# Encoder block on one core: operands of the first up-projection round split and ordered anew, down-projection loads chained

## The chip, the cores and the metric

The kernel runs on 1 core of one Trainium2 chip. The metric is the device time in microseconds (us) of one launch. The engines are named as in the profile: PE (TensorE, matmuls), PEld (its weight loads), DVE (VectorE), ACT (ScalarE), POOL (GpSimd) and SP (SyncE, which issues DMAs here).

## What is computed

One encoder block over 1024 tokens of width 1024: a token mixer (convolution group and attention group), a cross-attention into 256 memory tokens, and a gated MLP. The change lies in the last step of the cross-attention, in the gated MLP and in nothing ahead of them. Cut to that:

```python
# D_MODEL = 1024, SEQ = 1024, D_FF = 2816
y = memory_cross_attention(h, mem_n, w_mem_q, w_mem_kv, w_mem_o)
x = x + rmsnorm(y, norm_mem_post)
h = rmsnorm(x, norm_ffn_pre)
u = jnp.einsum("bsd,df->bsf", h, w_up)          # 1024 -> 2 * 2816
u = dwconv_centred(u, ffn_dw, ffn_dw_b)          # width 3 over tokens
gate, val = u[..., :D_FF], u[..., D_FF:]
y = jnp.einsum("bsf,fd->bsd", gelu(gate) * val, w_down)
x = x + rmsnorm(y, norm_ffn_post)
```

All is float32.

## The kernel before

**Products.** A float32 operand is split into a high half (a cast to the fp32r type, on ACT) and a low half (the operand less its high half, a subtraction on DVE or POOL). A product of two operands is three matmuls for each slice of 128 rows: high by high, high by low, low by high (`gemm3`, lines 98, 99 and 101). A `product` of the up projection is four slices, so 12 matmuls of 128x512.

**Cross-attention's last step.** A loop over eight tiles of 128 tokens, `t` = 0 to 7. `cross_gemm(t)` multiplies (the matmuls `y<-Uw,P`), `cross_norm(t)` makes two RMS norms: a square with a running sum on ACT (L621, then L725), a scale and a power on POOL (`rsqrt`, L86 and L87), a scale on DVE (L623, then L727) and, between the two norms, the residual's addition on DVE (L624). `cross_operands(t)` turns the result on PE (`pTs`) and stores it in tiles `r_b` for the up projection.

**Up projection.** It is done with seven products instead of eight (Strassen and Winograd), in 22 rounds `fi`. The weights of a round are loaded as `wg` and `wv`, sums of them (`s`, L813 to L816, on POOL) and their halves (`a`, L780 on ACT, L781 on POOL or DVE) are the operands on the left. The operands on the right are made once from the tokens: b11, b21 (tiles 0 to 3 of `t`), b22, t1, t2, t3, t4 (tiles 4 to 7), each with halves `h` and `l`. In `cross_operands(t)` for `t` = 4 to 7 each piece of 128 tokens is subtracted (L713) and split (L709, L710) on its own. t3 and t4 lie in the buffers of the raw b12 and b21. A round is `up_first` (products with b11 and b21), `up_operands` (the halves) and `up_finish` (t1, t2, b22, t3, t4, the convolution, the gate and the store of the result to `act_d`, L869). The products' sums are added on DVE (L805, L842); there are four PSUM buffers of that kind, and the next product waits until the addition has read its buffer. While round `fi` is finished, `down_sums` (L773, four subtractions of 128x256 each round, on DVE) makes sums of the down projection's weights.

**Down projection.** Seven products m1, m2, m6, m7, m5, m4, m3 over 11 slices `i`; each slice takes 12 matmuls `yd` (L91 to L93) with one operand tile `op`: the left part is cast from `acts` (the stored gate results, loaded at L903 and L906 to L908), the right part from `st`, which one DMA brings for two slices (L924). The buffer of `st` is taken in turn from the pool `raw` (3 buffers) and the pool `tmp` (4 buffers, shared with the sums `s` and the gate results `o`).

**What sets the order.** A scheduler orders the instructions of every engine from its own estimate of when each could run. `tc.issue_after(x)` ties the instructions inside it behind `x`; `tc.high_priority()` lets them go ahead.

Of the kernel before, what the change touches and what calls it, by code (L numbers as in the profile page):

```python
# [34 lines left out]
def encoder_block(ctx: ExitStack, tc: tile.TileContext, x, xT, mem, w_a, w_q, w_kv, w_mkv, w_mqT,  # L35
# [668 lines left out]

    def b_split(name, ts_):
# [3 lines left out]
        nc.scalar.copy(out=hi[:, :, ts_], in_=src[:, :, ts_])  # L709
        nc.vector.tensor_tensor(out=lo[:, :, ts_], in0=src[:, :, ts_], in1=f(hi[:, :, ts_]), op=ALU.subtract)  # L710
# [18 lines left out]

    def cross_operands(t, j):  # L730
        h, tt = t // 4, t % 4
# [47 lines left out]
    def a_split(dst, src, eng):  # L779
# [27 lines left out]

    def up_operands(fi):

        rg, u, q = firsts.pop(fi)  # L810
        rv = load_raw(w_up[fi, 1], "wv")
        s12, s34 = tmp("s12"), tmp("s34")
        nc.gpsimd.tensor_tensor(out=s12[:, H0], in0=rv[:, H0], in1=rv[:, H1], op=ALU.add)  # L813
        nc.gpsimd.tensor_tensor(out=s12[:, H1], in0=s12[:, H0], in1=rg[:, H0], op=ALU.subtract)
        nc.gpsimd.tensor_tensor(out=s34[:, H0], in0=rg[:, H0], in1=rv[:, H0], op=ALU.subtract)
        nc.gpsimd.tensor_tensor(out=s34[:, H1], in0=rg[:, H1], in1=s12[:, H1], op=ALU.subtract)  # L816
        a2, a3 = W([2, 2, 512], "a2"), W([2, 2, 512], "a3")
        a_split(a2[:, 0], s12[:, H1], nc.vector)
        a_split(a2[:, 1], s12[:, H0], nc.vector)
        a_split(a3[:, 0], s34[:, H1], nc.vector)  # L820
        lo = a_split(a3[:, 1], s34[:, H0], nc.vector)
# [50 lines left out]
    for t in range(8):
        if t == 6:
            for fi in range(UP_PRE):
                rgs[fi] = load_raw(w_up[fi, 0], "wg")
# [4 lines left out]
        cross_operands(t, j)  # L880
    for fi in range(NF + 1):
        if fi < NF:
# [3 lines left out]
            lo = up_operands(fi)  # L886
            down_load(fi)
        if fi:
            up_finish(fi - 1)
        else:  # L890
            down_sums(0, lo)
# [25 lines left out]
    def right(name, i):  # L917

        if i % 2 == 0:
# [199 lines left out]
```

## Time and profile of the kernel before

| | us |
|---|---|
| median of 3 runs | 1430.79 |
| lowest, highest | 1429.89, 1430.89 |
| the profiled execution: its time | 1431.57 |
| its span | 1429.8 |
| PE busy | 1376.8 (96% of the span) |
| DVE busy | 1099.9 (77%) |
| ACT busy | 699.5 (49%) |
| POOL busy | 527.1 (37%) |
| mean granted clock of PE, as a share | 0.988 |

The span is the profiled execution's stretch between the first and the last instruction; what lies around it is 1431.57 - 1429.8 = 1.77 us. In the views below a row of the timeline names a start, a duration, the engine, the line, the operation and the tiles (out<-in); in brackets stands how long the engine had been idle before, and whose work ended that. Rows of the same kind that follow each other are merged (x4). Matmuls overlap: one lasts longer than the distance to the next start.

### The profile page before, as it was taken

What the parts mean: (1) busy time and instruction counts of PE and PEld (TensorE: products, weight loads), DVE (VectorE), ACT (ScalarE), POOL (GpSimd) and SP (SyncE); (2) the same over time, 40 slices, a digit from 0 to 9 for tenths busy, and PEclk for the clock granted to TensorE, in tenths of its full rate; (3) what the DMA queues carried; (4) which work ended last, traced back from release to release, by engine and by line L of the source; (5) the groups of instructions that cost most, each with busy time, mean ns of one, the idle gap of its engine ahead of it and who ended that gap; (6) DMA issues with size and microseconds to landing.
All of it is one profiled execution on the core that took longest, in us unless ns stands there. A gap on an engine that the chain in (4) does not pass through costs nothing.

```text
span 1429.8 us, 18873 instructions
## 1 busy us (share of the span) xinstructions
PE 1376.8 (96%) x7042; PEld 1164.9 (81%) x7042; DVE 1099.9 (77%) x1443; ACT 699.5 (49%) x1190; POOL 527.1 (37%) x505
## 2 busy tenths in 40 slices
PE   9999999889999999999997999999999997999997
PEld 7889987679898888888885788888888886888885
DVE  6699899799999433435449989898898998696576
ACT  7426653678888444334335444444434444354452
POOL 5538877801011433102126455555555540000002
PEclk9999999999999999999998999999999998999998
DMA  7417760000000433203222443334444449523326
GB/s 239 138 50 230 244 224 14 21 1 1 30 1 1 148 104 133 74 32 116 88 89 88 162 147 133 121 130 147 133 147 147 148 148 331 212 82 96 103 89 213
DMA packets 77228, 170.08 MB, mean 119 GB/s; under 512 B 10065, under 2 KB 32849, under 8 KB 77137
## 3 DMA queue, kind: packets, MB, share of 16 engines
q1 hardware_dynamic: 77136, 168.88, 35.5%
q8 instruction: 55, 0.90, 0.2%
q14 instruction: 37, 0.30, 0.1%
HBM read 124.82 MB, written 44.04 MB: 118 GB/s over the span
## 4 chain that ended last, share of the span: by engine, by line
PE 69%; DVE 4%; DMA 2%; ACT 1%; issue 1%; POOL 1%; SPq 0%; POOLq 0%; DVEq 0%; ACTq 0%
PE p L101 9%; PE p L99 9%; PE p L98 9%; PE yd L91 5%; PE yd L92 5%; PE yd L93 5%; PE y L99 4%; PE y L101 4%; PE y L98 4%; PE pPT L82 3%; PE sc L101 2%; PE sc L98 2%; PE sc L99 2%; PE sp L536 2%; PE po L567 2%; PE sp L537 2%
## 5 line engine op out<-in xcount | busy, mean ns | idle before, releaser
L305 DVE SCALAR_TENSOR_TENSOR cacc<-conv,col,cacc 128x1009 f32<-128x1009 f32 (+14 forms) x120 | 145.8, 1275 | 4.8 <-ACT cacc L253 4.5
L86 POOL TENSOR_SCALAR rt<-ss 128x1 f32<-128x1 f32 (+1 forms) x43 | 14.9, 346 | 364.9 <-DVE ss L935 238.8
L92 PE MATMUL yd<-op 128*128 128x512 f32 x308 | 120.8, 393 | 0.0
L93 PE MATMUL yd<-op 128*128 128x512 f32 x308 | 120.6, 392 | 0.0
L91 PE MATMUL yd<-op 128*128 128x512 f32 x308 | 101.1, 393 | 9.1 <-ACT op L945 9.1
L945 ACT CAST op<-acts 128x512 fp32r<-128x512 f32 x77 | 47.8, 623 | 109.9 <-PE yd L93 99.5
L781 POOL TENSOR_TENSOR a<-wg,a 128x512 fp32r<-128x512 f32 x44 | 68.4, 1576 | 62.3 <-ACT a L780 62.3
L935 DVE TENSOR_TENSOR op<-acts,op 128x512 fp32r<-128x512 f32 x77 | 52.8, 688 | 46.7 <-ACT op L945 46.6
L781 DVE TENSOR_TENSOR a<-s,a 128x512 fp32r<-128x512 f32 x88 | 87.8, 1037 | 0.0
L831 ACT ACTIVATE c<-u,col 128x1024 f32<-128x1024 f32 x44 | 53.2, 1209 | 66.5 <-DVE u L842 66.5
L557 DVE TENSOR_TENSOR PL<-pPT,PH 128x512 fp32r<-128x512 f32 x128 | 83.1, 680 | 2.3 <-ACT PH L556 1.3
L539 DVE TENSOR_REDUCE nm<-sp 128x1 f32<-128x1024 f32 x64 | 78.0, 1218 | 7.4 <-PE sp L537 6.9
L780 ACT CAST a<-s 128x512 fp32r<-128x512 f32 x88 | 50.2, 619 | 64.8 <-DVE o L868 50.0
L842 DVE TENSOR_TENSOR u<-p,u 128x512 f32<-128x512 f32 x110 | 75.1, 683 | 7.2 <-PE p L101 6.2
L542 ACT ACTIVATE P<-sp,nm 128x1024 f32<-128x1024 f32 x64 | 72.1, 1126 | 15.4 <-PE pPT L82 6.5
L832 DVE SCALAR_TENSOR_TENSOR c<-u,col,c 128x1023 f32<-128x1023 f32 x44 | 56.5, 1285 | 28.8 <-ACT c L831 28.8
L556 ACT CAST PH<-pPT 128x512 fp32r<-128x512 f32 x128 | 69.4, 594 | 14.1 <-PE pPT L82 13.6
L91 PEld LDWEIGHTS yd<-op 128*128 128x128 f32 x308 | 58.5, 190 | 21.6 <-ACT op L945 9.5
L781 POOL TENSOR_TENSOR a<-wv,a 128x512 fp32r<-128x512 f32 x22 | 33.4, 1517 | 114.0 <-ACT a L780 112.9
L92 PEld LDWEIGHTS yd<-op 128*128 128x128 f32 x308 | 58.4, 190 | 12.7 <-DVE op L935 0.4
L82 PE MATMUL pPT<-ident,P 128*128 128x128 f32 x512 | 67.9, 273 | 0.7 <-DVE PL L557 0.7
L93 PEld LDWEIGHTS yd<-op 128*128 128x128 f32 x308 | 58.4, 190 | 12.2
(343 smaller groups left out, 4378.8 us busy)
## 6 DMA issues: line engine op xcount, KB each, us to landing
wg<-in_w_up_dram SPq DMA_DIRECT2D x22, 512.0 KB, 4.6
wv<-in_w_up_dram SPq DMA_DIRECT2D x22, 512.0 KB, 4.4
wd<-in_w_down_dram SPq DMA_DIRECT2D x22, 512.0 KB, 5.5
T_d<-wd SPq DMA_DIRECT2D x22, 512.0 KB, 3.2
act_d<-o SPq DMA_DIRECT2D x22, 512.0 KB, 3.1
acts<-act_d SPq DMA_DIRECT2D x44, 256.0 KB, 6.4
st<-T_d SPq DMA_DIRECT2D x20, 512.0 KB, 3.7
wmkv_r<-in_w_mkv_dram SPq DMA_DIRECT2D x16, 512.0 KB, 4.2
```

The source lines that it names most:

```text
L82: nc.tensor.transpose(out=out_, in_=in_, identity=ident)
L91: nc.tensor.matmul(out=ps, lhsT=sh, rhs=mh, start=first, stop=False)
L92: nc.tensor.matmul(out=ps, lhsT=sh, rhs=ml, start=False, stop=False)
L93: nc.tensor.matmul(out=ps, lhsT=sl, rhs=mh, start=False, stop=last)
L98: nc.tensor.matmul(out=p, lhsT=sh, rhs=mh, start=first, stop=False)
L99: nc.tensor.matmul(out=p, lhsT=sh, rhs=ml, start=False, stop=False)
L101: ins = nc.tensor.matmul(out=p, lhsT=sl, rhs=mh, start=False, stop=last)
L305: nc.vector.scalar_tensor_tensor(out=acc[:, t0:t1_], in0=a[:, t0 + o:t1_ + o], scalar=cc(C_DW + c * 31 + j), in1=acc[:, t0:t1_], op0=ALU.m ...
L539: nc.vector.reduce_max(out=nm, in_=sp, axis=AX.X, negate=True)
L557: nc.vector.tensor_tensor(out=PL[dst], in0=p3, in1=f(PH[dst]), op=ALU.subtract)
L781: return eng.tensor_tensor(out=dst[:, 1, :], in0=src, in1=f(dst[:, 0, :]), op=ALU.subtract)
L842: return nc.vector.tensor_tensor(out=dst, in0=other if swap else ps, in1=ps if swap else other, op=op)
```

## The change

**Right operands.** t3 and t4 are no longer split for each token tile. After the loop each is cast and subtracted once, on 128x2048, tied behind the last split of the others (t2's for the last tile). From `t` = 6 on the third subtraction (t3) goes to DVE instead of POOL.

**Left operands of the first rounds.** Round 0's weights are loaded at `t` = 3 and its sums made on POOL there. Round 1's go into a buffer `gv`. `up_weights`, `up_sums` and `up_seconds` are functions of their own; the low halves of rounds 0 and 1 on POOL are tied behind the last power of a norm, the `a2` halves behind the norm's square and scale. `cross_norm(7)` is made at high priority after round 0's `up_first`. Round 1's sums go to DVE, behind round 0's seventh product; `down_sums` of rounds 0 and 1 go behind round 0's gate.

**Down projection.** The loads of `st` are chained, each tied behind the load before it in the program. The first three take `raw` buffers, and from the fourth on odd ones take `raw` and even ones `tmp`.

```diff
+        last_pow[0] = nc.gpsimd.tensor_tensor(out=out_, in0=t, in1=mhalf[:, :n], op=ALU.pow)
...
     def cross_operands(t, j):
+        third = nc.gpsimd if t < 6 else nc.vector
...
-            b_sub("t3", "b22", "b12", ts_, nc.gpsimd)
+            b_sub("t3", "b22", "b12", ts_, third)
             b_sub("t2", "b22", "t1", ts_, nc.vector)
             b_split("t2", ts_)
-            b_split("t3", ts_)
             b_sub("t4", "t2", "b21", ts_, nc.vector)
-            b_split("t4", ts_)
...
+    def up_weights(fi, hi_at=None, lo_at=None):
         rg = rgs.pop(fi) if fi in rgs else load_raw(w_up[fi, 0], "wg")
         a1 = W([2, 2, 512], "a1")
-        a_split(a1[:, 0], rg[:, H0], nc.gpsimd)
-        a_split(a1[:, 1], rg[:, H1], nc.gpsimd)
+        a_split(a1[:, 0], rg[:, H0], nc.gpsimd, hi_at, lo_at)
+        a_split(a1[:, 1], rg[:, H1], nc.gpsimd, hi_at, lo_at)
+        weights[fi] = rg, a1
...
-        if fi + 1 < NF:
+        if 0 < fi < NF - 1:
             down_sums(fi + 1, seventh)
+        if fi == 0:
+            up_weights(2, last_hi[0])
+            with tc.issue_after(seventh.ins):
+                up_sums(1, firsts[1][0], nc.vector)
+                up_operands(1)
...
     UP_PRE = 2
+    PRE_T = 3
     for t in range(8):
-        if t == 6:
-            for fi in range(UP_PRE):
-                rgs[fi] = load_raw(w_up[fi, 0], "wg")
-        j = cross_norm(t, *cross_gemm(t))
-        if t == 7:
-            for fi in range(UP_PRE):
-                up_first(fi)
+        if t == PRE_T:
+            rgs[0], rvs[0] = load_raw(w_up[0, 0], "wg"), load_raw(w_up[0, 1], "wv")
+        y, xr = cross_gemm(t)
+        if t < 7:
+            j = cross_norm(t, y, xr)
+            if t == PRE_T:
+                up_sums(0, rgs[0])
+        else:
+            gv = wp.tile([128, 2, 1024], F32, tag="w", name="gv")
+            rgs[1], rvs[1] = gv[:, 0], gv[:, 1]
+            for i in range(2):
+                last_load[0] = nc.sync.dma_start(out=gv[:, i], in_=w_up[1, i])
+            up_weights(0, lo_at=last_pow[0])
+            up_first(0)
+            with tc.high_priority():
+                j = cross_norm(t, y, xr)
+            up_weights(1, lo_at=last_pow[0])
+            up_seconds(0, last_sq[0], last_h[0])
+            up_first(1)
         cross_operands(t, j)
...
-            lo = up_operands(fi)
+            if fi != 1:
+                up_operands(fi)
+            if fi == 0:
+                hi, lo = last_hi[0], last_lo[0]
+                with tc.issue_after(hi.ins), tc.issue_after(lo.ins):
+                    for n in ("t3", "t4"):
+                        b_split(n, slice(0, 512))
...
+        if fi == 1:
+            for n in range(2):
+                down_sums(n, gated)
...
-            st = (tmp if nst[0] % 2 == 0 else raw)("st").rearrange("p (i n) -> p i n", i=2)
-            ld = nc.sync.dma_start(out=st[:, :n, :], in_=src[i:i + n, :, b, :].rearrange("i p n -> p i n"))
-            pair[0] = st
+            st = (raw if nst[0] % 2 or nst[0] == 2 else tmp)("st").rearrange("p (i n) -> p i n", i=2)
+            with tc.issue_after(last_load[0].ins):
+                ld = nc.sync.dma_start(out=st[:, :n, :], in_=src[i:i + n, :, b, :].rearrange("i p n -> p i n"))
+            pair[0], last_load[0] = st, ld
```

The three places where the order of instructions moves, as the two programs issue them. (The numbers in tile names differ between the programs; `r_b_7058` before and `r_b_7068` after are t3's buffer, `r_b_6641` is t4's, `r_b_7059` and `r_b_7069` are t2's.)

DVE, end of the first round's operands, before (`a_7461`, `a_7462` are halves for round 0, `a_7487`, `a_7488` for round 1):

```order
L713 TENSOR_TENSOR r_b_7059<-r_b_7059,r_b_6640 128x4x128
L710 TENSOR_TENSOR t3l<-r_b_7058,t3h 128x4x128 x4
L713 TENSOR_TENSOR r_b_6641<-r_b_7059,r_b_6641 128x4x128
L781 TENSOR_TENSOR a_7462<-s_7456,a_7462 128x512
L710 TENSOR_TENSOR t2l<-r_b_7059,t2h 128x4x128
L710 TENSOR_TENSOR t4l<-r_b_6641,t4h 128x4x128 x4
L781 TENSOR_TENSOR a_7487<-s_7481,a_7487 128x512 x2
L781 TENSOR_TENSOR a_7488<-s_7482,a_7488 128x512 x2
L842 TENSOR_TENSOR u<-p_7500,u 128x512
```

The same place after (`a_7447` holds halves for round 0, `s_7529` and `s_7530` are round 1's sums):

```order
L714 TENSOR_TENSOR t1l<-r_b_6640,t1h 128x4x128
L717 TENSOR_TENSOR r_b_7069<-r_b_7069,r_b_6640 128x4x128
L820 TENSOR_TENSOR u<-p_7398,u 128x512
L717 TENSOR_TENSOR r_b_6641<-r_b_7069,r_b_6641 128x4x128
L714 TENSOR_TENSOR t2l<-r_b_7069,t2h 128x4x128
L790 TENSOR_TENSOR a_7447<-s_6978,a_7447 128x512 x2
L714 TENSOR_TENSOR t3l<-r_b_7068,t3h 128x2048
L873 TENSOR_TENSOR u<-p_7465,u 128x512
L714 TENSOR_TENSOR t4l<-r_b_6641,t4h 128x2048
L873 TENSOR_TENSOR u<-p_7466,u 128x512
```

The four pieces of t3l stood ahead of t2l and of the rest; now t2l and round 0's halves come first, t3l and t4l are one instruction each, and round 1's sums and halves stand behind them.

POOL, last token tile and first round, before:

```order
L713 TENSOR_TENSOR r_b_7058<-r_b_7059,r_b_7058 128x4x128
L781 TENSOR_TENSOR a_7393<-wg,a_7393 128x512 x2
L86 TENSOR_SCALAR rt_7355<-ss 128x1
L87 TENSOR_TENSOR rs<-rt_7355,mhalf 128x1
L813 TENSOR_TENSOR s_7455<-wv 128x512
L815 TENSOR_TENSOR s_7456<-wg,wv 128x512
L814 TENSOR_TENSOR s_7455<-s_7455,wg 128x512
L713 TENSOR_TENSOR r_b_7058<-r_b_7059,r_b_7058 128x4x128
L816 TENSOR_TENSOR s_7456<-wg,s_7455 128x512
```

and after (`a_7334` is round 0's, `a_7386` round 1's left operand for b11 and b21):

```order
L790 TENSOR_TENSOR a_7334<-wg,a_7334 128x512 x2
L88 TENSOR_SCALAR rt_7372<-ss 128x1
L89 TENSOR_TENSOR rs<-rt_7372,mhalf 128x1
L88 TENSOR_SCALAR rt_7382<-ss 128x1
L89 TENSOR_TENSOR rs<-rt_7382,mhalf 128x1
L790 TENSOR_TENSOR a_7386<-gv,a_7386 128x512 x2
L790 TENSOR_TENSOR a_7452<-wv,a_7452 128x512
L790 TENSOR_TENSOR a_7452<-gv,a_7452 128x512
L790 TENSOR_TENSOR a_7524<-wg,a_7524 128x512 x2
```

Round 1's low halves (before `a_7393`, ahead of the last norm's second power) now stand behind both powers of the last norm; the eight sums of rounds 0 and 1 that stood here are gone from it.

SP, last rounds of the up projection, before (`st_10612`, issued 29 rows earlier, is m1's first load; `st_10648` its second, `st_10726` its fourth, `st_10845` m2's first):

```order
L924 DMA st_10845<-in_w_down_dram 128x2x512
L906 DMA acts_10598<-act_d_6642 128x512
L869 DMA act_d_6642<-o_10494 128x1024
L910 DMA gF_10604<-in_rows_dram 128x1024
L907 DMA acts_10598<-act_d_6642 128x512
L908 DMA acts_10598<-act_d_6642 128x512
L907 DMA acts_10600<-act_d_6642 128x512
L907 DMA acts_10602<-act_d_6642 128x512
L906 DMA acts_10600<-act_d_6642 128x512
L908 DMA acts_10600<-act_d_6642 128x512
L924 DMA st_10648<-in_w_down_dram 128x2x512
L924 DMA st_10726<-in_w_down_dram 128x2x512
```

and after (`st_10635` is m1's second load, `st_10671` its third):

```order
L982 DMA st_10599<-in_w_down_dram 128x2x512
L960 DMA acts_10569<-act_d_6642 128x512
L780 DMA T_d_6643<-wd_6644 512x1x256
L960 DMA acts_10571<-act_d_6642 128x512
L960 DMA acts_10573<-act_d_6642 128x512
L960 DMA acts_10575<-act_d_6642 128x512
L905 DMA act_d_6642<-o_10336 128x1024
L982 DMA st_10635<-in_w_down_dram 128x2x512
L982 DMA st_10671<-in_w_down_dram 128x2x512
```

m1's second load stood behind its third, its fifth and m2's first, and behind the next to last store to `act_d`; now it follows its first with six rows between and stands ahead of the last two stores. ACT, at the end of m1 after (`op_10843`, `op_10863`, `op_10885` are m2's first three operands, `u_10593` m1's result; before, three whole operands of m2 stood ahead of these copies):

```order
L1003 CAST op_10843<-acts_10569 128x512
L1003 CAST op_10805<-st_10797 128x512
L1003 CAST op_10863<-acts_10571 128x512
L1003 CAST op_10885<-acts_10573 128x512
L1070 COPY u_10593<-yd_10595 128x512
L1070 COPY u_10593<-yd_10596 128x512
L1070 COPY u_10593<-yd_10597 128x512
L1070 COPY u_10593<-yd_10598 128x512
L1003 CAST op_10905<-acts_10575 128x512
L1003 CAST op_10843<-st_10832 128x512
L1003 CAST op_10863<-st_10832 128x512
```

The casts from `st` for m2's first operands stand behind the four copies of m1's result.

## Rows read from the trace of the kernel before

**Rows 1.** Page, part 1: busy time, share of the span, instructions of each engine.

```profile
PE 1376.8 (96%) x7042; PEld 1164.9 (81%) x7042; DVE 1099.9 (77%) x1443; ACT 699.5 (49%) x1190; POOL 527.1 (37%) x505
```

**Rows 2.** Waits of PE from 740 to 842 us: whom for, total, times, longest.

```profile
PE p L99 <- DVE t3l L710: 3.8, 1, 3.8
PE pTs L82 <- DVE h L727: 3.4, 2, 2.3
PE p L98 <- ACT t1h L709: 3.1, 1, 3.1
PE p L99 <- DVE t1l L710: 1.9, 1, 1.9
```

**Rows 3.** Windows: from:to, us, busy of PE, PEld, DVE, ACT, POOL; PEclk, DMA share, GB/s.

```profile
756.01:841.00 84.99, 71.74 (x295) 56.72 (x294) 79.30 (x89) 40.01 (x64) 51.81 (x37) 0.90 0.37 124
1197.40:1419.00 221.60, 212.50 (x926) 175.03 (x924) 158.03 (x258) 98.19 (x183) 10.40 (x13) 0.98 0.44 150
```

**Rows 4.** Timeline of PE, first round of the up projection.

```profile
757.45 1.06 PE L82 MATMUL pTs<-ident,h 128*128 128x128 f32 x8 [1.06 <-DVE h L727]
758.27 0.48 PE L98 MATMUL p<-b11h,a 128*128 128x512 f32 x1
...
763.84 0.39 PE L98 MATMUL p<-b11h,a 128*128 128x512 f32 x1
...
789.00 0.80 PE L99 MATMUL p<-t3l,a 128*128 128x512 f32 x1 [3.82 <-DVE t3l L710]
...
793.86 0.63 PE L101 MATMUL p<-b22h,a 128*128 128x512 f32 x1
```

**Rows 5.** A window of the same stretch, columns as in rows 3.

```profile
788.00:792.00 4.00, 3.00 (x7) 2.42 (x8) 4.00 (x3) 2.99 (x6) 3.70 (x3) 0.50 0.42 131
```

**Rows 6.** Timeline of DVE, from the cross loop's end to round 1.

```profile
749.17 2.32 DVE L624 TENSOR_TENSOR x<-x,x1r 128x1024 f32<-128x1024 f32 x1
...
762.84 1.83 DVE L710 TENSOR_TENSOR b22l<-r_b,b22h 128x512 fp32r<-128x512 f32 x1
764.59 1.78 DVE L710 TENSOR_TENSOR t1l<-r_b,t1h 128x512 fp32r<-128x512 f32 x1
766.29 1.21 DVE L624 TENSOR_TENSOR x<-x,x1r 128x1024 f32<-128x1024 f32 x1
...
783.21 5.73 DVE L710 TENSOR_TENSOR t3l<-r_b,t3h 128x512 fp32r<-128x512 f32 x4
...
793.03 2.50 DVE L710 TENSOR_TENSOR t4l<-r_b,t4h 128x512 fp32r<-128x512 f32 x4
...
824.86 2.41 DVE L773 TENSOR_TENSOR wd<-wd 128x256 f32<-128x256 f32 x2
```

**Rows 7.** Timeline of ACT: the square of the last norm.

```profile
758.47 1.02 ACT L621 ACTIVATE x<-y 128x1024 f32<-128x1024 f32 x1
```

**Rows 8.** Timeline of POOL: round 1's low halves, the last norm's second power.

```profile
762.83 2.99 POOL L781 TENSOR_TENSOR a<-wg,a 128x512 fp32r<-128x512 f32 x2
...
769.44 0.95 POOL L87 TENSOR_TENSOR rs<-rt,mhalf 128x1 f32<-128x1 f32 x1
```

**Rows 9.** Timeline of PE: first yd, the stop in m1, last yd.

```profile
1197.47 0.39 PE L91 MATMUL yd<-op 128*128 128x512 f32 x1
...
1212.15 2.08 PE L91 MATMUL yd<-op 128*128 128x512 f32 x4 [9.08 <-ACT op L945]
...
1418.92 0.39 PE L93 MATMUL yd<-op 128*128 128x512 f32 x1
```

**Rows 10.** Timeline of ACT: casts from st in m1, copies of m1's result.

```profile
1211.48 1.14 ACT L945 CAST op<-st 128x512 fp32r<-128x512 f32 x2 [3.49 <-DMA st<-in_w_down_dram]
...
1237.84 2.26 ACT L1012 COPY u<-yd 128x512 f32<-128x512 f32 x4
```

**Rows 11.** Timeline of SP: two loads of st, the last store to act_d.

```profile
1205.33 1.14 SPq L924 DMA_DIRECT2D st<-in_w_down_dram  x2
...
1208.86 0.32 SPq L869 DMA_DIRECT2D act_d<-o  x1
```

**Rows 12.** Tile st, 1190 to 1240 us: its loads from issue to landing.

```profile
DMA to landing us min/median/max: 3.7/7.0/8.0
```

More of the change, by code (lines that the diff above doesn't have):

```diff
@@ L708, in b_split @@
         src, (hi, lo) = BR[name], BO[name]
-        nc.scalar.copy(out=hi[:, :, ts_], in_=src[:, :, ts_])
-        nc.vector.tensor_tensor(out=lo[:, :, ts_], in0=src[:, :, ts_], in1=f(hi[:, :, ts_]), op=ALU.subtract)
+        last_hi[0] = nc.scalar.copy(out=hi[:, :, ts_], in_=src[:, :, ts_])
+        last_lo[0] = nc.vector.tensor_tensor(out=lo[:, :, ts_], in0=src[:, :, ts_], in1=f(hi[:, :, ts_]), op=ALU.subtract)
     def b_sub(dst, in0, in1, ts_, eng):
@@ L777, in down_store, with a_split @@
             nc.sync.dma_start(out=down_slice(T_d, fi), in_=wd_b[:, fi % 2])
-    def a_split(dst, src, eng):
+    def a_split(dst, src, eng, hi_at=None, lo_at=None):
+        if lo_at is not None:
+            with tc.issue_after(lo_at.ins):
+                return a_split(dst, src, eng, hi_at)
+        if hi_at is not None:
+            with tc.issue_after(hi_at.ins):
+                return a_split(dst, src, eng)
         nc.scalar.copy(out=dst[:, 0, :], in_=src)
@@ L806, in up_first, with up_sums, up_seconds @@
         firsts[fi] = (rg, u, q)
+    rvs, sums, seconds = {}, {}, {}
+    def up_sums(fi, rg, eng=None):
+        eng = eng or nc.gpsimd
+        rv = rvs.pop(fi) if fi in rvs else load_raw(w_up[fi, 1], "wv")
+        s12, s34 = tmp("s12"), tmp("s34")
+        eng.tensor_tensor(out=s12[:, H0], in0=rv[:, H0], in1=rv[:, H1], op=ALU.add)
+        eng.tensor_tensor(out=s12[:, H1], in0=s12[:, H0], in1=rg[:, H0], op=ALU.subtract)
+        eng.tensor_tensor(out=s34[:, H0], in0=rg[:, H0], in1=rv[:, H0], op=ALU.subtract)
+        eng.tensor_tensor(out=s34[:, H1], in0=rg[:, H1], in1=s12[:, H1], op=ALU.subtract)
+        sums[fi] = rv, s12, s34
+    def up_seconds(fi, hi_at=None, lo_at=None):
+        if fi not in sums:
+            up_sums(fi, firsts[fi][0])
+        s12 = sums[fi][1]
+        seconds[fi] = a2 = W([2, 2, 512], "a2")
+        a_split(a2[:, 0], s12[:, H1], nc.vector, hi_at, lo_at)
+        a_split(a2[:, 1], s12[:, H0], nc.vector, hi_at, lo_at)
     def up_operands(fi):
+        if fi not in seconds:
+            up_seconds(fi)
         rg, u, q = firsts.pop(fi)
[L811 to L821, printed above, removed]
+        rv, _, s34 = sums.pop(fi)
+        a2, a3 = seconds.pop(fi), W([2, 2, 512], "a3")
+        hi_at, lo_at = (last_hi[0], last_lo[0]) if fi == 0 else (None, None)
+        a_split(a3[:, 0], s34[:, H1], nc.vector, hi_at, lo_at)
+        lo = a_split(a3[:, 1], s34[:, H0], nc.vector, hi_at, lo_at)
         if fi % 2 == 0:
             a22[0] = W([2, 2, 512], "a22")
-        a_split(a22[0][:, fi % 2], rv[:, H1], nc.gpsimd)
+        a_split(a22[0][:, fi % 2], rv[:, H1], nc.gpsimd, hi_at)
         ups[fi] = (a2, a3, a22[0][:, fi % 2], u, q)
@@ L885, in encoder_block @@
                 down_store(fi - 2)
[L886 removed]
+            if fi != 1:
[5 more added lines that the diff above has]
+                        b_split(n, slice(0, 512))
             down_load(fi)
         if fi:
[L889 to L891 removed]
+            gated = up_finish(fi - 1)
+        if fi == 1:
+            for n in range(2):
+                down_sums(n, gated)
     for fi in (NF - 2, NF - 1):
```

17 lines of the change are left out of this document (11 added, 6 removed).

## The prediction

> **What bounds the kernel now.** I read the busy times first: PE has work in 96% of the span [rows 1], so nothing on another engine is worth a microsecond unless PE waits for it. Next the waits of PE: the longest in the kernel is one of 9.08 us at the start of the down projection [rows 9], and four kinds between 740 and 842 us add up to 3.8 + 3.4 + 3.1 + 1.9 = 12.2 us, all of them for operands of the first up-projection round [rows 2]. These are the two stretches that the change touches. A stop costs more than its idle time, so I count each stretch as a whole.
>
> At full clock twenty-four matmuls start in 763.84 - 758.27 = 5.57 us, 0.23 us each [rows 4]; over the down projection it is 0.227. First window [rows 3]: 84.99 us for 295 entries, 16 of them transposes (eight take 1.06 us, so a start every 0.10 [rows 4]). 279 x 0.227 + 16 x 0.10 = 64.9 us of work, so **20.0 us are lost in the first rounds**. After a long stop PE restarts at half clock: the window from 788 us has a granted clock of 0.50 [rows 5], which is the lower level, 1.2 GHz, and from 789.00 to 793.86 PE needed 4.86 us for some eleven matmuls [rows 4], about 0.43 each. That is 0.2 us more per matmul, about 2.4 us after a stop of this length.
>
> From the first to the last `yd` pass 1418.92 - 1197.47 = 221.45 us [rows 9]; 924 matmuls (the window's 926 less two of the up projection [rows 3]) need 209.5. **12.0 us are lost in the down projection**: the 9.08, about 2.4 of half clock after it, 0.5 elsewhere.
>
> **First round, what goes.** In before PE stood 3.82 us for t3l because its four pieces took 5.73 us [rows 4, 6] and waited for one another's casts. Now one subtraction of 128x2048 is made. Four pieces that nothing slowed took 2.50 us [rows 6]; one instruction should take a little less, 2.3. With POOL at work DVE is slower: 128x1024 took 2.32 instead of 1.21, and pieces of 128x512 took 1.8 instead of 0.6 [rows 6]. Both widths lose 1.1 to 1.2 us, so the loss goes with the number of instructions and not with the width; that gives 3.4 us for the wide one at worst. If it went with the width, 5.73 us. I count from the first t1 product (zero). DVE then has t1l, three short ones, t2l and two halves, about 5 us with the waits for ACT's casts, so t3l ends at 7.3 to 8.4 us, t4l at 10.5 to 12.5. PE has 36 matmuls ahead of t3's product (8.2 us) and 48 ahead of t4's (10.9), and the low halves are wanted one matmul later. So the wait is 0 to 1.4 us, I take 0.3; with 5.73 us each, t3l and t4l together cost about 5.
>
> The Trainium skill, page "SBUF — State Buffer", section "SBUF: two separate sides", says that a VectorE instruction with two SBUF inputs and a GpSimd instruction that reads SBUF take turns on a shared pair of ports, which is "an exclusive lock, not a bandwidth split", held for the whole instruction. By that rule one wide instruction waits once where four waited four times. The equal loss at both widths agrees with it.
>
> The waits for t1h and t1l (3.1 and 1.9 us [rows 2]) go too: the last tile's transposes now stand between round 1's two products, and ten matmuls of work (2.3 us) cover the copy, the subtraction and the cast. I take nothing for them; the 0.3 above is for all of it.
>
> **First round, what comes.** (i) Round 1's low halves on POOL now stand behind the last norm's second power. In before ACT began that norm's square at 758.47 [rows 7] and the power ended at 769.44 + 0.95 = 770.39 [rows 8]. On the way DVE had two subtractions of 1.83 and 1.78 us in front of the residual's addition [rows 6], slowed because POOL was making these very halves (762.83, 2.99 us for two [rows 8]). Now POOL is idle there and two subtractions take 1.2 us: 2.4 less, so 768.0, and the first half is ready 1.5 us later [rows 8], at 769.5. PE leaves round 0's products at 763.84 [rows 4] and has four matmuls of round 1 that need high halves only: 764.7. The stop is 4.8 us. If ACT takes the square as soon as the matmuls end, two us earlier, and POOL's small steps are quicker, it is 2.4; if DVE loses the 2.4 again, 7.2. I take 4.5, and 2.4 for half clock behind it.
>
> (ii) The wait of 1.06 us ahead of the first transposes [rows 4] stays.
>
> (iii) `down_sums` of rounds 0 and 1 and the halves for later rounds now stand on DVE in front of the addition that frees a PSUM buffer for round 3's product with b21: the addition of t3's product, two halves, two `wd`, then the addition itself. POOL works all through this. By 1.43 us for a half (5.73 / 4) and 1.2 for a `wd` (2.41 / 2) [rows 6] that is 0.6 + 5.3 + 0.6 = 6.5 us; PE has t4's twelve matmuls and two more, 3.2 us. The stop is 3.3 us, with nothing slowed by POOL zero, with every one at 1.8 it is 4.5. I take 3.3 and 2.0 of half clock.
>
> (iv) Round 0's loads and sums move to `t` = 3. PE waited there for none of DVE or POOL; an extra DVE loss of 1.1 us is covered by the next tile's 48 matmuls. Zero, at most 1.
>
> Lost after: 0.3 + 4.5 + 2.4 + 1.1 + 3.3 + 2.0 + 0.4 for the starts behind stops = 14.0 us, against 20.0: **gain 6.0**.
>
> **Down projection.** ACT waited for `st` until 1211.48, for a load that SP issued at 1205.33 [rows 10, 11], by the order behind seven loads of `acts`, one of `gF` and a store; it is m1's second, which m1's third and fifth and m2's first had overtaken. It now has a `raw` buffer at once and stands in front of the last two stores. The fourth is issued in front of the last store, the fifth two `acts` loads behind it: 1208.86 [rows 11] + 1.5 = 1210.4, landed 3.7 to 8.0 us later [rows 12], cast by 1219.5 at the latest. PE needs it after eight slices, 1197.47 + 8 x 12 x 0.227 = 1219.3. So m1 runs through.
>
> What is late next is m2. Its casts from `st` stand behind the four copies of m1's result, 2.26 / 4 = 0.57 us each [rows 10]. The first three can be made while PE ends m1; the last starts with m1's end, and behind it come a cast of `acts` and one of `st` (1.14 for two [rows 10]) and the low half. PE stops 2.2 us. Before m2's third slice a second stop can come, if its load is late: zero by the landing times above (over 4 us to spare), 3.5 by the longest wait of ACT on a landing [rows 10]; the loads are chained and stand behind more `acts` loads, so I take 1.5. Half clock for a short while, 1.0, and 1.0 elsewhere (0.5 more than before). Lost after 5.7 against 12.0: **gain 6.3**. Behind the last `yd` nothing changes.
>
> Sum: 12.3 us off the profiled execution's 1431.57 (span 1429.8 and 1.8 around it). That execution is 0.8 above the median of 1430.79, so on the median 1430.8 - 12.3 = 1418.5 us.
>
> **Rivals.** (A) The forecast, both gains within their bounds: 1412 to 1422, at 1418.5. (B) The up projection gives nothing, because the tie of (i) costs 7.2 us and t3l and t4l, slowed with their width, still come 2 to 3 us late: 20.0 lost again, 1430.8 - 6.3 = 1424.5. The width-free loss in rows 6 speaks against it. The change would then not have done what it says. (C) The down projection gives next to nothing: the chain puts later loads behind one late one, and m2 or m1 waits 6 us: 1430.8 - 6.0 - 0.5 = 1424. Against it: fewer loads wait for a `tmp` buffer. (D) Neither (iii) nor the second stop in m2 arises, since DVE and DMA have room: 12.3 + 5.3 + 2.5 = 20.1 off, 1410.7. (E) Slower: after the stop at (i) PE does not get back to full clock, because in these rounds further stops follow it closely. Each matmul then costs 0.2 us more; the gain of 12.3 is used up after 62 matmuls at half clock beyond those that I count, and the two first rounds have 168: +33.6 - 12.3 = 21.3, 1452. In every stretch of before the clock came back after some twelve matmuls, which speaks against it.
>
> **How the numbers follow.** A 0.65, B 0.14, C 0.10, D 0.08, E 0.03. The forecast is A's, 1418.5. A to D reach from 1410 to 1425; both gains at their worse bounds give 1426. Leaving out E, half of D and the edges of B and C, 1410 to 1425.5 should hold 8 in 10. A measurement tells 0.2% (2.9 us) from no change. Faster by more than that is all of A, B, C and D but for 0.04 in which B and C come together: 0.93; same 0.04; slower 0.03.
>
> **What would show it.** Right: no wait of PE for t3l or t4l above 1 us, one t3l of 2.3 to 3.5 us; a wait for POOL's `a` (L790) of 3 to 6 us with a granted clock of 0.50 behind it; a wait of 2 to 5 us on the L873 addition before round 3's product with b21; no wait above 1 us in m1; one near 2 us at m2's start on ACT's `op`. Wrong: t3l at 5 us or more (loss by width), a stop at (i) above 7 us, an ACT wait on `st` above 3 us in m1 or m2, or half clock for more than 25 matmuls on end.

## Result and profile after

| | before | after |
|---|---|---|
| median, us (runs) | 1430.84 (6) | 1422.53 (6) |
| lowest, highest | 1428.96, 1433.23 | 1421.75, 1424.38 |
| the profiled execution | 1431.57 | 1421.75 |
| its span | 1429.8 | 1419.9 |

The ratio is 0.9943, with a 95% interval from 0.9931 to 0.9955: the change makes the kernel 8.2 us faster (6.4 to 9.9). Forecast were 1418.5 us, 12.3 us faster, and a range of 1410 to 1425.5. The direction and the range held; a third of the forecast gain did not come.

The page of the changed kernel, part 1:

```profile
PE 1374.8 (97%) x7042; PEld 1163.3 (82%) x7042; DVE 1096.8 (77%) x1443; ACT 698.8 (49%) x1184; POOL 520.4 (37%) x499
```

The waits of PE from 740 to 842 us (answers to [rows 2]) and from 1185 to 1425 us:

```profile
PE p L100 <- DVE u L873: 4.7, 1, 4.7
PE p L103 <- POOL a L790: 4.5, 1, 4.5
PE p L100 <- ACT a L789: 0.5, 1, 0.5
PE p L101 <- DVE t1l L714: 0.5, 1, 0.5
...
PE yd L93 <- ACT op L1003: 3.0, 2, 1.8
PE yd L94 <- DVE op L993: 1.1, 2, 0.6
```

All four waits of [rows 2] are gone or down to 0.5 us, and so is the stop of 9.08 us in [rows 9]. In their place stand two new long ones, for POOL's low halves and for an addition on DVE, and short ones in the down projection: two for ACT at m2's start (1.81 and 1.23 us, at 1224.56 and 1231.92) and two for DVE in the product behind it (0.63 and 0.49 us, at 1264.03 and 1273.06).

The first rounds, from the start of the last cross matmul to the end of the same stretch of the up projection (columns as in rows 3), and the two new stops on PE's timeline:

```profile
755.22:836.17 80.95, 70.82 (x295) 56.76 (x294) 74.59 (x90) 39.10 (x58) 41.75 (x28) 0.92 0.36 117
```

```profile
768.31 0.79 PE L103 MATMUL p<-b11h,a 128*128 128x512 f32 x1 [4.49 <-POOL a L790]
...
772.31 0.63 PE L103 MATMUL p<-b11h,a 128*128 128x512 f32 x1
...
814.64 0.76 PE L100 MATMUL p<-b21h,a 128*128 128x512 f32 x1 [4.65 <-DVE u L873]
...
820.33 0.57 PE L101 MATMUL p<-t2l,a 128*128 128x512 f32 x1
```

The stretch took 84.99 us in before [rows 3] and takes 80.95: 4.0 us gained. From its end to the last `yd` pass 1418.92 - 841.00 = 577.9 us in before and 1408.42 - 836.17 = 572.25 after: 5.7 gained. Behind the last `yd` 10.9 became 11.5: 0.6 lost. The last cross matmul started at 756.01 in before and at 755.22 after; that 0.8 us lies ahead of everything the change moves (the transposes at 673.60 in before and 672.81 after, 80 us earlier, are as far apart), and in the profiled executions of the experiments the same point lies anywhere from 754.5 to 759.0. Sum: 4.0 + 5.7 - 0.6 + 0.8 = 9.9, the difference of the spans. Without the 0.8 it is 9.1, near the 8.2 of all runs.

### The profile page after: what moved, and what is told of

The parts are those of the page before. It is cut to its first block, busy times and chain, and to the rows that moved or that the text cites. A ratio compares the mean times of both kernels' runs of the same rounds, so it can differ in the third digit from the quotient of the medians.

```text
span 1419.9 us, 18862 instructions
## 1 busy us (share of the span) xinstructions
PE 1374.8 (97%) x7042; PEld 1163.3 (82%) x7042; DVE 1096.8 (77%) x1443; ACT 698.8 (49%) x1184; POOL 520.4 (37%) x499
## 5 line engine op out<-in xcount | busy, mean ns | idle before, releaser
L88 POOL TENSOR_SCALAR rt<-ss 128x1 f32<-128x1 f32 (+1 forms) x43 | 13.9, 322 | 355.8 <-DVE ss L993 234.2
L94 PE MATMUL yd<-op 128*128 128x512 f32 x308 | 120.3, 391 | 1.3 <-DVE op L993 1.1
L95 PE MATMUL yd<-op 128*128 128x512 f32 x308 | 119.6, 389 | 0.0
L93 PE MATMUL yd<-op 128*128 128x512 f32 x308 | 97.7, 390 | 3.0 <-ACT op L1003 3.0
L558 ACT CAST PH<-pPT 128x512 fp32r<-128x512 f32 x128 | 69.4, 594 | 14.1 <-PE pPT L82 13.6
```

Source lines behind the costliest of these rows:

```text
L93: nc.tensor.matmul(out=ps, lhsT=sh, rhs=mh, start=first, stop=False)
L94: nc.tensor.matmul(out=ps, lhsT=sh, rhs=ml, start=False, stop=False)
L95: nc.tensor.matmul(out=ps, lhsT=sl, rhs=mh, start=False, stop=last)
L558: nc.scalar.copy(out=PH[dst], in_=p3)
```

## Experiments

Each ratio is against runs of the kernel before on the same chip, with its 95% interval; the last column is the ratio on 1430.8 us.

| kernel | median | ratio | us against before |
|---|---|---|---|
| changed kernel | 1422.53 | 0.9943 (0.9931 to 0.9955) | -8.2 |
| e1_down_only | 1427.82 | 0.9975 (0.9965 to 0.9985) | -3.6 |
| e2_up_only | 1427.35 | 0.9970 (0.9960 to 0.9981) | -4.3 |
| e3_sums_behind | 1418.75 | 0.9911 (0.9898 to 0.9924) | -12.7 |
| e4_untied | 1419.77 | 0.9920 (0.9906 to 0.9935) | -11.4 |
| e5_pieces | 1417.05 | 0.9903 (0.9889 to 0.9916) | -13.9 |
| e6_lo_early | 1420.56 | 0.9929 (0.9912 to 0.9946) | -10.2 |
| e7_m2_early | 1417.98 | 0.9905 (0.9888 to 0.9922) | -13.6 |
| e8_sums_untied | 1421.08 | 0.9927 (0.9914 to 0.9940) | -10.4 |
| e9_three | 1423.85 | 0.9954 (0.9937 to 0.9971) | -6.6 |
| e10_sums_pieces | 1425.89 | 0.9965 (0.9951 to 0.9979) | -5.0 |
| e11_after_again | 1423.61 | 0.9951 (0.9934 to 0.9968) | -7.0 |
| e12_sums_again | 1419.06 | 0.9918 (0.9898 to 0.9938) | -11.7 |

### The two halves apart

e1: the kernel before with the new loads of `st`. e2: the changed kernel with the old ones.

```diff
-            st = (tmp if nst[0] % 2 == 0 else raw)("st").rearrange("p (i n) -> p i n", i=2)
-            ld = nc.sync.dma_start(...)
+            st = (raw if nst[0] % 2 or nst[0] == 2 else tmp)("st").rearrange("p (i n) -> p i n", i=2)
+            with tc.issue_after(last_load[0].ins):
+                ld = nc.sync.dma_start(...)
```

> The kernel before with the new chain and buffers of the loads of st alone. Theory (the two halves of the change are worth 4 to 6 us each and do not depend on each other): no stop of 9 us in m1, two short stops at the start of m2, 5 to 6.5 us faster than before, 1424 to 1426. Rival (the down projection's stop in before came from the late up projection, so the chain gives little by itself): the stop in m1 stays above 5 us, less than 2 us faster.

> The changed kernel with the loads of st as they were before. Theory: the first rounds give 4 us, the stop in m1 of about 9 us is back, 3 to 5 us faster than before, 1426 to 1428. Rival (the gain of the first rounds is given back further on, by a later stop): within 1.5 us of before.

Alone they gave 3.6 and 4.3 us, together 7.9, beside 8.2 (and 7.0 in the second measurement) for both: the halves add up. In e1 the stop in m1 is gone, though the up projection in front of it is as late as in before; in e2 it is back, a little longer. PE's waits for ACT from 1170 us on, of e1, then of e2:

```profile
PE yd L91 <- ACT op L946: 3.0, 2, 1.8
```

```profile
PE yd L93 <- ACT op L1002: 10.5, 1, 10.5
```

So the loads of `st` alone made the stop, and the rival that the late up projection did is out. e1 and e2 change the chain and the buffers of the loads together; which of the two it takes is not shown. e1's time fell short of what was expected for it (5 to 6.5 us).

### The addition behind the weights' sums

e3 takes the eight subtractions of rounds 0 and 1 out of the way of the addition that frees the PSUM buffer, and places them behind round 1's seventh product.

```diff
+        if fi == 1:
+            for n in range(2):
+                down_sums(n, seventh)
...
         if fi:
-            gated = up_finish(fi - 1)
-        if fi == 1:
-            for n in range(2):
-                down_sums(n, gated)
+            up_finish(fi - 1)
+        if fi == 2:
+            down_store(0)
+            down_load(2)
```

> The changed kernel with the weights' sums of rounds 0 and 1 (eight subtractions of 128x256 on DVE) behind round 1's seventh product instead of behind round 0's gate; round 0's store and round 2's load of those weights move behind them. Theory (the 4.65 us stop of PE before round 3's product with b21 is DVE's queue: eight wd subtractions stand in front of the addition that frees the PSUM buffer): the stop falls under 1 us, the half clock behind it goes, 5 to 7.5 us faster than the changed kernel, 1415 to 1418. Rival (the stop comes from POOL slowing DVE and from the halves that remain in front): the stop stays above 2.5 us with half clock behind it, less than 3 us faster.

The stop of 4.65 us went, with its half clock, and the kernel was 4.6 and 4.7 us faster than the changed one, on two chips (0.9911 beside 0.9943, and 0.9918 beside 0.9951). That is less than the 5 to 7.5 expected. PE's timeline in e3 shows where the rest went: to stops at the starts of rounds 5 to 7, 2.8 us in all, that the changed kernel does not have.

```profile
848.20 0.50 PE L100 MATMUL p<-b11h,a 128*128 128x512 f32 x1 [1.09 <-ACT a L789]
...
890.47 0.50 PE L103 MATMUL p<-b11h,a 128*128 128x512 f32 x1 [1.00 <-POOL a L790]
```

PE that is not stopped in one place comes earlier to the next, before the halves for it are there: round 5 starts at 848.20 in e3, at 855.19 in the changed kernel. DVE works almost without a pause in both. Here is the window of the first of these stops in e3, then that of the long stop in the changed kernel, in which PE does nothing while DVE and POOL are both full (columns as in rows 3):

```profile
846.00:850.00 4.00, 2.86 (x11) 1.56 (x11) 4.00 (x6) 2.27 (x3) 2.86 (x3) 1.00 0.98 312
```

```profile
810.00:814.00 4.00, 0.00 (x0) 0.00 (x0) 4.00 (x4) 0.10 (x1) 4.00 (x4) 0.98 0.39 131
```

### The tie of round 1's low halves

e4 is the changed kernel without the tie, e8 is e3 without it.

```diff
-            up_weights(1, lo_at=last_pow[0])
+            up_weights(1)
```

> The changed kernel with round 1's low halves on POOL no longer tied behind the last norm's second power; POOL then makes them between the norm's two powers, and PE turns the last tile after round 1's second product instead of in front of its last ten matmuls. Theory (the tie costs the 4.5 us stop and 2.1 us of half clock, but without it the norm is later by 2 to 2.5 us and PE waits for the turned tile and for t1 instead, with half clock behind that): no POOL wait in round 1, stops of 4 to 6 us in all at the transposes and t1, within 2 us of the changed kernel. Rival 1 (the tie is a pure loss): 5 to 7 us faster. Rival 2 (the tie pays): over 2 us slower.

> The kernel with the weights' sums behind round 1's seventh product, and round 1's low halves not tied behind the norm's power. Theory (untying gained 3.6 us over the changed kernel only because PE came later and POOL was then idle beside the sums that stood in front of the addition, so the later stop fell away): with the sums moved, untying gives nothing more, 1417.5 to 1420.5. Rival (untying is worth 3 to 4 us by itself in the first rounds): 1414 to 1416.

In both, the POOL stop fell to 0.4 us and PE waited instead for the turned tile and for t1, as in e8's timeline:

```profile
770.65 1.09 PE L82 MATMUL pTs<-ident,h 128*128 128x128 f32 x8 [1.56 <-DVE h L731]
774.91 0.80 PE L100 MATMUL p<-t1h,a 128*128 128x512 f32 x1 [3.16 <-ACT t1h L713]
776.26 0.79 PE L101 MATMUL p<-t1l,a 128*128 128x512 f32 x1 [0.55 <-DVE t1l L714]
```

With the short waits for `a` (0.52 and 0.37 us) that is 6.2 us in the first rounds, against 5.4 in e3 with the tie (4.5, 0.5 and 0.4): the tie saves 0.7 us there. e8 stands 2.3 us behind e3, at 0.9927 against 0.9911 (the intervals meet; expected was no difference), and most of that is another stop, which e3 does not have. PE waits for a DVE addition that stands behind two `wd`; they took 2.82 us with POOL at work (from 808.49 on) and 0.75 in e3, where POOL was idle until 807.63:

```profile
808.68 2.82 DVE L776 TENSOR_TENSOR wd<-wd 128x256 f32<-128x256 f32 x2
...
813.35 0.50 PE L100 MATMUL p<-t2h,a 128*128 128x512 f32 x1 [1.69 <-DVE u L873]
```

Yet e4 was 3.3 us faster than the changed kernel, more than expected (the intervals just meet), because the later stop of 4.65 us did not come. The same instructions stand in front of the addition in both. Here is the end of t3's product on PE in the changed kernel, then DVE in the changed kernel, from the addition of the product before it to the addition that PE waits for, then DVE in e4 from the half on:

```profile
806.43 0.39 PE L103 MATMUL p<-t3h,a 128*128 128x512 f32 x1
```

```profile
807.63 0.68 DVE L873 TENSOR_TENSOR u<-p,u 128x512 f32<-128x512 f32 x1
808.23 1.18 DVE L790 TENSOR_TENSOR a<-s,a 128x512 fp32r<-128x512 f32 x1
809.34 1.50 DVE L776 TENSOR_TENSOR wd<-wd 128x256 f32<-128x256 f32 x1
810.75 1.74 DVE L790 TENSOR_TENSOR a<-s,a 128x512 fp32r<-128x512 f32 x1
812.42 1.48 DVE L776 TENSOR_TENSOR wd<-wd 128x256 f32<-128x256 f32 x1
813.82 0.68 DVE L873 TENSOR_TENSOR u<-p,u 128x512 f32<-128x512 f32 x1
```

```profile
808.98 0.67 DVE L790 TENSOR_TENSOR a<-s,a 128x512 fp32r<-128x512 f32 x1
809.58 0.41 DVE L776 TENSOR_TENSOR wd<-wd 128x256 f32<-128x256 f32 x1
809.91 0.68 DVE L790 TENSOR_TENSOR a<-s,a 128x512 fp32r<-128x512 f32 x1
810.51 0.41 DVE L776 TENSOR_TENSOR wd<-wd 128x256 f32<-128x256 f32 x1
810.85 0.67 DVE L873 TENSOR_TENSOR u<-p,u 128x512 f32<-128x512 f32 x1
```

And POOL beside them, in the changed kernel, then in e4:

```profile
807.56 2.98 POOL L790 TENSOR_TENSOR a<-wg,a 128x512 fp32r<-128x512 f32 x2 [2.34 <-ACT a L789]
810.51 1.44 POOL L790 TENSOR_TENSOR a<-wv,a 128x512 fp32r<-128x512 f32 x1
```

```profile
806.15 1.68 POOL L790 TENSOR_TENSOR a<-wv,a 128x512 fp32r<-128x512 f32 x1 [3.97 <-ACT a L789]
810.49 3.29 POOL L790 TENSOR_TENSOR a<-wg,a 128x512 fp32r<-128x512 f32 x2 [2.66 <-ACT a L789]
```

The four instructions take 5.6 us with POOL at work and 1.9 us with POOL idle until 810.49. This difference is 3.7 of the 4.65 us. POOL's halves come when ACT has cast `wg`, and ACT casts it when PE has ended t3's product: at 806.86 in the changed kernel and at 809.79 in e4. So where PE comes later, POOL does too, and DVE is through in front of it. In e4 PE began t4's product 2.9 us later than in the changed kernel (809.59 for 806.66) and DVE the half 0.75 us later; two microseconds of shift between them decide whether the stop comes.

### Pieces instead of one wide subtraction

e5 is the changed kernel, e10 is e3, with t3 and t4 split in four pieces each.

```diff
-                        b_split(n, slice(0, 512))
+                        for c in range(4):
+                            b_split(n, slice(c * 128, c * 128 + 128))
```

> The changed kernel with t3 and t4 split after the loop in four pieces of 128x512 each (cast and subtraction) instead of one of 128x2048; same place, same tie. Theory (DVE's loss beside POOL goes with the number of instructions): the eight subtractions take 7 to 11 us instead of 5.1, PE waits 1 to 4 us for t3l or t4l, and what follows shifts; 1 to 5 us slower than the changed kernel, unless the shift moves POOL off the later stop. Rival (the loss goes with the width, the pieces only let PE start earlier): t3l and t4l together within 1 us of 5.1, no stop there, the same time.

> The kernel with the weights' sums behind round 1's seventh product, with t3 and t4 split in four pieces of 128x512 instead of one of 128x2048. Theory (pieces cost PE a stop near 1.6 us for t4l, and the changed kernel with pieces was fast only because POOL was idle beside the sums in front of the addition): 0.5 to 2.5 us slower than the kernel with the sums moved alone on the same chip. Rival (the pieces are worth something by themselves): over 1 us faster than it.

DVE and POOL in the changed kernel, then in e5:

```profile
781.44 2.29 DVE L714 TENSOR_TENSOR t3l<-r_b,t3h 128x2048 fp32r<-128x2048 f32 x1 [1.06 <-ACT t3h L713]
...
784.25 2.79 DVE L714 TENSOR_TENSOR t4l<-r_b,t4h 128x2048 fp32r<-128x2048 f32 x1
```

```profile
782.00 2.89 POOL L790 TENSOR_TENSOR a<-gv,a 128x512 fp32r<-128x512 f32 x1 [0.46 <-ACT a L789]
784.85 4.59 POOL L790 TENSOR_TENSOR a<-wg,a 128x512 fp32r<-128x512 f32 x2
```

```profile
780.94 2.49 DVE L714 TENSOR_TENSOR t3l<-r_b,t3h 128x512 fp32r<-128x512 f32 x4
...
784.08 2.77 DVE L714 TENSOR_TENSOR t4l<-r_b,t4h 128x512 fp32r<-128x512 f32 x2
...
787.37 2.85 DVE L714 TENSOR_TENSOR t4l<-r_b,t4h 128x512 fp32r<-128x512 f32 x2
```

```profile
780.32 4.28 POOL L790 TENSOR_TENSOR a<-wv,a 128x512 fp32r<-128x512 f32 x1 [9.26 <-ACT a L789]
```

The eight pieces took 8.1 us, the two wide ones 5.1, and PE waited 1.6 us for t4l in e5 and e10 alike. So the loss does not go with the width. It needs POOL to come in between, too: t3l's four pieces, back to back, took 2.49 us and lost nothing, t4l's four took 5.6.

And yet e5 was 5.7 us ahead of the changed kernel. POOL's next halves came after the sums in front of the addition (its `a<-wg` at 812.24 instead of 807.56), and of the stop of 4.65 us 0.65 was left. PE and DVE were both later than in the changed kernel, by nearly as much (t4's product by 2.6 us, the half by 2.1), but on ACT the casts of `wg` now stood behind an activation `c` that waits for DVE; in the changed kernel they stood in front of it (806.86, then `c` at 808.35):

```profile
810.41 1.21 ACT L862 ACTIVATE c<-u,col 128x1024 f32<-128x1024 f32 x1 [4.49 <-DVE u L873]
811.56 1.12 ACT L789 CAST a<-wg 128x512 fp32r<-128x512 f32 x2
```

PE had ended t3's product, for which the cast of `wg` waits, at 809.39, so in the old order POOL would have come about 2 us earlier (an estimate; no run has the pieces with ACT's old order). With the sums out of the way the kernel with pieces is the slower one: e10 is 6.8 us slower than e12 on the same chip, by the 1.6 us and by a stop of 3.92 us in a later round that neither theory foresaw. There ACT waited for a load of `wv` and cast `wg`, which PE needed, behind it:

```profile
854.18 0.62 ACT L789 CAST a<-wv 128x512 fp32r<-128x512 f32 x1 [1.95 <-DMA wv<-in_w_up_dram]
854.71 1.14 ACT L789 CAST a<-wg 128x512 fp32r<-128x512 f32 x2
```

In e12 ACT waited for the same load nearly as long (1.71 us, cast at 853.18), but `wg` was cast in front of it, at 850.34, and PE's stop was 1.18 us. So the load was no later in e10; the scheduler had put the two casts in another order. Of the 6.8 us only the 1.6 us stop is shown to be the pieces' own.

The Trainium skill, page "SBUF — State Buffer", section "SBUF: two separate sides", has the shared ports go to whichever instruction starts first, for its whole length. These rows agree: against t3l's wide subtraction, which had started first, it was POOL that waited (2.89 us, beside 1.29 alone); t4l's, which started while POOL was at work, lost 0.5 us; and a half and t3l's four pieces, back to back on DVE until 783.43, kept one of POOL's for 4.28 us.

### Other ways around the last norm

e6 is e3 with round 1's halves made ahead of the last norm; e9 also puts round 2's first two products in front of the last tile.

```diff
             up_weights(0, lo_at=last_pow[0])
+            up_weights(1, lo_at=last_pow[0])
             up_first(0)
             with tc.high_priority():
                 j = cross_norm(t, y, xr)
-            up_weights(1, lo_at=last_pow[0])
```

> The kernel with the weights' sums behind round 1's seventh product, and round 1's left halves made before the last norm (their POOL halves right behind round 0's, in the 3 us in which POOL stood idle before that norm's first power). Theory (the 4.5 us stop is only the tie; POOL has room ahead of the norm, so the norm is hardly delayed): no POOL wait in round 1; the norm itself, some 11 us from the last cross matmul to the scaled tile, is then what PE waits for, 2 to 4 us in all at the transposes and t1; 2 to 5 us faster than with the sums moved alone (1418.7), so 1414 to 1417. Rival (DVE and POOL then collide ahead of the norm, which comes later by the 2.4 us that the halves cost): stops of 5 us or more, 1417.5 to 1420.

> The kernel with the weights' sums behind round 1's seventh product and round 1's left halves made ahead of the last norm, and in addition round 2's first two products (24 matmuls, 5.4 us) in front of the last tile's operands; round 2's low halves are tied behind the last norm's power. Theory (whatever is tied, PE waits some 5 us in the first rounds because the last norm takes longer than the products of rounds 0 and 1; only more work for PE covers it): the 2.5 us wait for the turned tile and the 2.3 us wait for t1h go, no wait above 1.5 us there, 3 to 6 us faster than the same kernel without round 2's products, 1414.5 to 1417.5. Rival (DVE and POOL bound these rounds: PE only meets the same queues later): the stops come back within the next two rounds, within 2 us of 1420.5.

PE's stops in e6:

```profile
773.81 1.97 PE L82 MATMUL pTs<-ident,h 128*128 128x128 f32 x8 [2.54 <-DVE h L731]
...
778.06 0.79 PE L100 MATMUL p<-t1h,a 128*128 128x512 f32 x1 [2.29 <-ACT t1h L713]
779.41 0.79 PE L101 MATMUL p<-t1l,a 128*128 128x512 f32 x1 [0.56 <-DVE t1l L714]
```

They add up to 5.4 us, as much as e3's; the rival held. e6 stands 2.6 us behind e3 (the intervals meet), with the same later stop of 1.69 us as e8, behind two `wd` of 2.82 us. Four placings of the low halves (e3, e4, e6, e8) all cost PE 5.4 to 6.2 us there: the chain from the last cross matmul through two norms to the turned tile is longer than the products of two rounds. In e9 the wait for the turned tile went, but PE then waited 0.9 us for POOL's low halves, 1.84 and 0.5 us for t1, and 2.31 us for a cast at 799.39: the stops came back as in the rival, and at 0.9954 e9 is no faster than e6 (0.9929; the intervals meet).

### The start of m2

e7 is e3 with m2's first two operands cast ahead of the copies of m1's result, and each cast from `st` ahead of that from `acts`.

```diff
+            hi = nc.scalar.copy(out=op[:, 2, :], in_=t_)
+            with tc.issue_after(hi.ins):
+                nc.scalar.copy(out=op[:, 0, :], in_=s_)
...
     def done1(tt, p):
-        nc.scalar.copy(out=Y["u"][:, tt, :], in_=p)
+        with tc.issue_after(first_hi[1].ins):
+            nc.scalar.copy(out=Y["u"][:, tt, :], in_=p)
```

> The kernel with the weights' sums behind round 1's seventh product, and on ACT in the down projection: m2's first two operands cast ahead of the four copies of m1's result, and in m2 each cast from st ahead of the cast from acts. Theory (both stops at m2's start, 1.81 and 1.23 us, are the order on ACT: the copies, and casts from acts that wait for a tile PE still reads): both stops go, 2.5 to 4 us faster than with the sums moved alone (1418.7), so 1415 to 1416.5. Rival (the loads of st for m2 land late): an ACT wait on st takes the place of the stops, within 1 us of 1418.7.

ACT in the changed kernel, then in e7:

```profile
1221.42 2.05 ACT L1070 COPY u<-yd 128x512 f32<-128x512 f32 x4 [0.74 <-PE yd L95]
...
1230.73 0.62 ACT L1003 CAST op<-acts 128x512 fp32r<-128x512 f32 x1 [2.10 <-PE yd L95]
```

```profile
1219.25 0.62 ACT L1010 CAST op<-st 128x512 fp32r<-128x512 f32 x1 [5.81 <-DMA st<-in_w_down_dram]
...
1226.65 0.62 ACT L1010 CAST op<-st 128x512 fp32r<-128x512 f32 x1 [3.27 <-DMA st<-in_w_down_dram]
```

In the changed kernel the casts from `st` stood behind the copies and behind casts of `acts` that waited for a tile PE still read. With that order mended ACT waited 5.81 and 3.27 us for the loads themselves, and PE's two stops went from 1.81 + 1.23 to 0.90 + 1.64 us, while the two waits for DVE in the product behind m2 grew from 0.63 + 0.54 in e3 to 1.78 + 1.15. The theory that the order is the whole cause fell and the rival held: the loads themselves come too late. 0.9905 beside 0.9911 is no difference.

### Controls

> The changed kernel once more, as the measure for its neighbours on the same chip: 7 to 9.5 us faster than before if a run on another chip tells the same, and again a stop near 4.6 us before round 3's product with b21 with POOL at work beside it.

> The kernel with the weights' sums behind round 1's seventh product once more, beside the changed kernel and the four pieces on the same chip: 3 to 5.5 us faster than the changed kernel by the first measurement.

e11 was 7.0 us faster than before, at the lower end of what was expected, again with 4.66 us of stop at the addition; e12 was 4.7 us (0.9918 beside 0.9951) ahead of e11.

## Why the prediction was right, and which terms were off

**The bound and the losses** were read rightly: both stretches gave time, and nothing else did.

**(i) The tie**: forecast 4.5 us and 2.4 of half clock; measured 4.49, and ten matmuls at 0.43 us from 768.31 to 772.7, 2.0 us. The path was as told: the power ended at 766.88, the first half was there when PE went on at 768.31. The upper bound (DVE losing again) did not come. A cast made PE wait 0.5 us ahead of it, which no term had.

**(ii)** The 1.06 us ahead of the first transposes [rows 4] were to stay; they went. I had given no reason for that term, and had overlooked that round 0's low halves are tied as well. In before POOL made them (750.38, 3.98 us) in front of the power (755.04) that the scaled tile waits for; in the changed kernel the power came first (752.26) and they followed (752.78). That they went is luck for the sum: it hides half of what (iii) cost over its term.

**(iv)** Zero, as forecast: from the transposes at 710.28 (709.49 after) to the last cross matmul it is 45.73 us in both.

**t3 and t4**: forecast 0.3 us; measured none, 0.46 for t1l in all. The wide subtractions took 2.29 and 2.79 us, under the 3.4 allowed: for t3l POOL waited for DVE, not DVE for POOL. They ended 7.8 and 11.1 us after the first t1 product, inside the bounds. e5 showed what pieces cost there, 8.1 us for 5.1. One reading was wrong: in before t3l's pieces did not wait for one another's casts, which had ended at 778.7; DVE ran them without a gap from 783.21, with POOL at work beside them throughout.

**(iii) The PSUM buffer** is the term that was mis-sized: 3.3 us and 2.0 of half clock; measured 4.65, and thirteen matmuls at 0.43, 2.6 us, and the starts. The mechanism, DVE's queue in front of the addition, was as told (e3). The prices were nearly right: the four instructions took 5.6 us for 5.3. The step that failed is when the queue starts. I let it start with the addition of t3's product, as soon as that product ends (806.82). But the addition at 807.63 is that of the product before, which PE had ended at 804.10 (in e4, with the same order on DVE, it starts at 808.38, before t3's product ends at 809.76); DVE was that far behind, with two more `wd` in front. The addition of t3's product is the one at the end of the queue, and it frees the buffer. So DVE started 0.8 us later than the sum has it: 0.8 + 0.6 + 5.6 + 0.7, and 0.1 until PE starts, less PE's 3.2, is 4.6. The bound given, 4.5 us, was nearly met; the other end, zero, is near what e4 and e5 got (none and 0.65).

Up projection: forecast 6.0, measured 4.0. With 0.4 us for all starts behind stops I was also too low: waits of 10.1 us and half clock of 4.6 explain 14.7 of the 80.95 - 64.9 = 16.0 lost, and the four starts behind stops take most of the other 1.3. Against the 14.0 of the sum: (iii) 2.0 more, the starts 0.9, the cast 0.5, t1l 0.2, (ii) 1.1 less and (i) 0.4 less.

**Down projection**: forecast 6.3, measured 5.7, and 0.6 lost behind the last `yd`, where I had said that nothing changes (it comes with the new loads: 11.7 in e1, and in e2, with the old ones, 10.6; why is open). m1 ran through, as forecast, though one sign that I had named as wrong came, a wait of ACT for `st` above 3 us, while PE had work:

```profile
1210.65 1.14 ACT L1003 CAST op<-st 128x512 fp32r<-128x512 f32 x2 [3.57 <-DMA st<-in_w_down_dram]
```

At m2's start came 1.81 us for 2.2 and 1.23 for 1.5; the half clock of 1.0 did not come in this execution (granted clock 1.00 in every window from 1220 to 1238). That was luck: the same stops were followed by seven or eight matmuls at 0.43 us in the traces of e1, e4, e6, e8, e10 and e12, here e8:

```profile
1224.00:1228.00 4.00, 4.00 (x13) 3.17 (x12) 3.43 (x7) 0.62 (x1) 0.00 (x0) 0.60 1.05 388
```

What was lost elsewhere, 1.0 in the sum, was 3.2 (215.8 us from the first to the last `yd`, less 209.5 and the two stops); 1.1 of it are the two waits for DVE behind m2, which no term had. For the second stop I named late loads; in the changed kernel ACT's casts of `acts` stood in front, and e7 showed that the loads were late as well.

The rivals: A in its mechanism, with a median 0.5 us outside its own bounds (1422). B needed a tie at 7.2 and t3l late, neither came; C no; D is what e4 and e5 show for (iii), though not because DVE has room: because POOL came later; E no, the clock was back after ten to thirteen matmuls each time.

## What to carry to other kernels

Where an engine is full in a stretch, removing one stop of PE moves part of it to the next queue (in e3 4.65 us and 2.6 of half clock went, and 4.6 were gained): measure the gain at the end of the stretch, not at the stop. Price an instruction that may meet POOL at both its prices, and give a stop that hangs on several of them its two ends, since a shift of two microseconds chooses between them. The kernel that moves the weights' sums behind the addition is the version to keep (two measurements, 11.7 and 12.7 us faster than before); e5, with the pieces, is not clearly faster than e3 (0.9903 and 0.9911; the intervals overlap), and what it gained hangs on where the scheduler put ACT's casts.

## What was not expected of the hardware

A wide subtraction on DVE came through in 2.29 us, what its width gives by the lone prices of 128x512 and 128x1024 (0.68 and 1.21), with POOL's 128x512 beside it at 2.89 instead of 1.29. Behind the stops of 4.49 and 4.65 us the granted clock was 0.50 for ten and thirteen matmuls. Behind a stop of 1.81 us it stayed at 1.00 in the traces of the changed kernel, e3, e9 and e11, and fell for seven or eight matmuls in those of e1, e4, e6, e8, e10 and e12: the same stop had its price in some executions and not in others.
